# Half-unit products in the opening's pauses and a sixth projection unit among the row groups of a hybrid decoder block

## The chip, the cores and the metric

The kernel runs on one core of one Trainium2 chip. The metric is the device time of one execution in microseconds (us), smaller is better. Beside three timed executions there is one profiled execution, from which all durations of single instructions come. Engines are named as in the profile: PE (TensorE products), PEld (its weight loads), DVE (VectorE), ACT (ScalarE), POOL (GpSimd), SP (SyncE, whose queue issues nearly all loads).

## The reference

The block takes x (256 rows of 2048) and a condition vector c (2048), in float32. Cut to what matters here:

```
mod = silu(c) @ w_ada + b_ada                       # 6 vectors of 2048
sh1, sc1, g1, sh2, sc2, g2 = split(mod, 6)
h = rms_norm(x, norm_mix_g) * (1 + sc1) + sh1
u, q, k, v, ga, gb = split(h @ w_in, ...)           # 4 x 1024, then 2 x 2048
y_ssm = s5_branch(u, ...)                           # scan, gelu, sigmoid(y @ w_glu)
y_att = moba_attention(q, k, v, rel_bias)           # here plain causal, 8 heads of 128
merged = sigmoid(ga) * (y_ssm @ w_proj_ssm) + sigmoid(gb) * (y_att @ w_proj_attn)
x = x + g1 * (merged @ w_out)
h2 = rms_norm(x, norm_mlp_g) * (1 + sc2) + sh2
x = x + g2 * (square(relu(h2 @ w_ff1)) @ w_ff2)
out = rms_norm(x, norm_final_g)
```

## The kernel before, in words

**Products.** Every large product splits each operand into a rounded part (hi) and the rest (lo) and adds three products: hi·hi, hi·lo and lo·hi. A weight tile of 128 rows and 1024 columns (512 KB) is loaded into wraw (7 places), rounded by ACT into whi and subtracted by DVE into wlo (4 places each; `load`, `split` and `stream`, lines 148 to 182). `gemm_t` (L184) uses the weights as the stationary operand and makes transposed results, 24 products of 256 columns for each tile. `gemm_n` (L219) uses the activations as the stationary operand and makes 12 products of 512 columns. Each such unit of 1024 output columns takes four banks of PSUM; the main pool has five (tag mm), a second pool three (tag ax).

**The rows of h.** The 2048 rows of the transposed h come 128 at a time (kt 0 to 15). Each row tile needs its part of sh1 and sc1, that is 256 columns of w_ada. For kt 0 to 3 PE makes these sums from specially laid out tiles (`ada_first`, L247: adap, then adac). For kt 4 to 15 DVE multiplies rows of w_ada by the broadcast vector cb and sums them (`ada_wide`, L326, L342: 128x2048 each). The loads of those go into a ring of places, four at first, later two, because half of the ring's space is taken by the scan's tables. `scale1` and `make_h1` (L460 to L472) then make h, and split it into ah (hi and lo).

**Order.** The kernel writes its order by hand. A unit is one of u, q, k, v and the gate halves (ga, gb), over one or more row groups: GR = (4, 6, 6) row tiles. In the first group (4 tiles) the units q, k, v and u run; then the first half of ga over groups 0 and 1, then u, v, k over group 1, q over groups 1 and 2, ga's first half and u over group 2 (the loop over `qkvu`, L1118). After that come k and v over group 2, then the second half of ga and both halves of gb over all 16 tiles, in single units. Partial sums of a unit are copied out by ACT the first time and added by DVE later. In the opening, q's four tiles run one row at a time: between two of them the sums of the next row are made (`follow`, L989), and then `idle` (L124) issues 8 products of 256 columns into a tile called unread, while the next row of h is being made.

**Lanes.** After each weight tile `step` advances the lanes, lists of smaller jobs, each at a rate in jobs per tile: w_ada's remaining sums (lane ada; rates R1 to R4, RS0 to RS3, RPA, RWO, RM), the building of the scan's tables (lane ssm; it begins after SL steps, rates SR1 and SR2), attention and then the scan itself (lane m; RAT and RSS). `want` and `drain` pull jobs of the lane ada ahead where rows are needed. Within this order a planner puts instructions by their priority and its own estimate of when they are ready. Each engine then carries out its list in that order.

**Places.** The tile x holds the transposed input until all rows of h are made. Then its slot (X16) becomes ga, both halves. The attention scores (asc) use free columns of ga. The slot S3 holds uT, the u unit's result, which 32 small DMAs on POOL's queue re-lay into u (`hop_in`, L807); afterwards S3 holds the scan's states. The bias table tz of attention is loaded by 4 DMAs on the same queue (`bias_load`, L499). When the scan is done, 32 more DMAs (`hop_out`) bring its result into yT, which is split into yy (hi and lo) for the product with w_glu.

Of the kernel before, what the change touches and what calls it, by code (L numbers as in the profile page):

```python
# [12 lines left out]
F32 = mybir.dt.float32  # L13
F32R = mybir.dt.float32r
# [5 lines left out]
P = 128  # L20
# [22 lines left out]
SR1 = .27  # L43
# [3 lines left out]
SL = 18  # L47
R1 = .92
R2 = .56
R3 = .15  # L50
R4 = .5
RS0 = 1.0
RS1 = 1.0
RSM = .1
# [4 lines left out]
RSS = .37  # L59
RPA = .69  # L60
# [17 lines left out]
class Kern:  # L78
    def __init__(self, ctx, tc, a, out):
# [9 lines left out]
        self.last = self.gate = self.hgate = self.agate = None  # L89
        self.gates = []  # L90
# [33 lines left out]
    def idle(self, n):  # L124
        o = self.aux("unread")[:, 0:S]
        for _ in range(n):
            with self.after(self.adac):
                self.nc.tensor.matmul(o, self.whi[:, 0:P], self.whi[:, 0:S], start=True, stop=True)
# [35 lines left out]

    def stream(self, src, kts, c0, homes=()):
        homes = list(homes)
        for kt in kts:
            with self.tc.high_priority(offset=OFF):
                w = self.load(src, kt, c0)
                home = homes.pop(0) if homes else None  # L170
                if home:
                    hi, lo = home
                else:
                    hi = self.wp.tile([P, 1024], F32R, name="whi", tag="whi", bufs=4)
                    lo = self.wp.tile([P, 1024], F32R, name="wlo", tag="wlo", bufs=4)
                self.gate, self.hgate = self.gates.pop(0) if self.gates else (None, None)
                self.split(hi, lo, w)
                self.gate = self.hgate = None
            if not isinstance(kt, list):
                self.want(kt)  # L180
            yield kt, hi, lo
            self.step()
# [64 lines left out]
    def ada_first(self, j, kt, done, home=None, gate=None):  # L247
# [29 lines left out]
        def fold(gate=None):  # L277
# [3 lines left out]
            done(pc[:, 0:1])  # L281
# [622 lines left out]
    def body(self):  # L904
# [64 lines left out]
        with self.tc.high_priority(offset=OF1):  # L969
# [9 lines left out]
            self.make_h1(0, A1, B1, 1)  # L979
            self.gates = [(None, self.acopy)]  # L980
# [7 lines left out]

        def follow(kt):  # L989
            def f():  # L990
                with self.tc.high_priority(offset=OF1):
                    parts = modn(kt, homes[kt], (self.mid, self.mm))
# [3 lines left out]
                    self.scale1(kt, n=1)  # L996
                    totals(parts)
                    self.idle(8)
                    self.make_h1(kt, A1, B1, 1)
# [522 lines left out]
```

## Time and profile before

| | |
|---|---|
| timed executions | 1396.94, 1400.31, 1401.72 us; median 1400.31 |
| profiled execution | 1400.28 us; span 1398.5 us from first to last instruction |
| granted clock of TensorE, mean over the span | 0.997 |
| busy: PE, DVE, ACT | 98%, 76%, 50% of the span |
| idle before products for rows of h (ah), 22 to 300 us | 4.9 us in 4 waits |
| loaded from memory | 350.79 MB, 253 GB/s over the span |

A row of the timeline gives start, duration, engine, line, operation, out<-in and shape; in brackets stands how long the engine was idle before it and what ended that. Products overlap in PE's pipeline, so the time from one start to the next says more than the duration. A row of the waits gives who waited for whom, total us, times and the longest.

### The profile page before, as it was taken

Reading aid. Unit: us, or ns where it says so; the run is one execution under the profiler, and the core shown is the slowest. Engines: PE = TensorE matmul, PEld = TensorE weight load, DVE = VectorE, ACT = ScalarE, POOL = GpSimd, SP = SyncE. Lnnn points to the kernel's source line nnn. Section 1 sums busy time; section 2 is a strip of 40 time slices with the busy share of each in tenths; the row PEclk is TensorE's granted clock in tenths of the full one; section 3 lists DMA queues with packets and bytes.
Section 4 is the critical chain, followed back from the end, with each engine's and each line's share of the span. In section 5 each row is a group of like instructions: output and inputs, shape, how many; then the busy total and the mean of one; then the engine's idle time right before and its main releaser. Section 6 shows DMA issues by size and latency. Waiting matters only on the chain.

```text
span 1398.5 us, 22052 instructions
## 1 busy us (share of the span) xinstructions
PE 1365.9 (98%) x8584; PEld 1179.5 (84%) x8584; DVE 1062.1 (76%) x1485; ACT 701.7 (50%) x928; POOL 42.5 (3%) x95
## 2 busy tenths in 40 slices
PE   6999999999999999999999999999999999999997
PEld 5888988978788897888999888888888888888885
DVE  5799998888798888977886976767666454555677
ACT  4554444346646743445455664544453553635543
POOL 1000000400002200000000000000000000000000
PEclk9999999999999999999999999999999999999999
DMA  9999965889356889898597877798878666566552
GB/s 373 392 405 342 330 222 167 236 291 340 125 157 212 286 285 351 286 351 283 198 381 276 310 244 246 250 251 286 242 238 241 199 194 189 188 190 188 181 195 75
DMA packets 112425, 356.47 MB, mean 255 GB/s; under 512 B 12240, under 2 KB 12272, under 8 KB 111904
## 3 DMA queue, kind: packets, MB, share of 16 engines
q1 hardware_dynamic: 109280, 348.96, 73.6%
q0 software_dynamic: 2896, 5.83, 1.4%
q8 instruction: 67, 1.10, 0.3%
q14 instruction: 38, 0.31, 0.1%
q10 hardware_dynamic: 144, 0.26, 0.1%
HBM read 350.79 MB, written 2.51 MB: 253 GB/s over the span
## 4 chain that ended last, share of the span: by engine, by line
PE 88%; DVE 6%; DMA 3%; ACT 2%; issue 1%; SPq 0%; DVEq 0%; ACTq 0%
PE pn L239 16%; PE pn L240 15%; PE pn L241 15%; PE pd L213 13%; PE pd L215 7%; PE pt L196 5%; PE pt L197 5%; PE pt L198 5%; DVE wlo L161 2%; DMA wraw<-in_w_proj_ssm_dram 1%; DVE wraw L300 1%; ACT whi L159 1%; PE trv L668 1%; PE ys L886 1%; PE rk L702 1%
## 5 line engine op out<-in xcount | busy, mean ns | idle before, releaser
L159 ACT CAST whi<-wraw 128x1024 fp32r<-128x1024 f32 x448 | 467.6, 1051 | 564.8 <-PE pn L240 247.4
L161 DVE TENSOR_TENSOR wlo<-wraw,whi 128x1024 fp32r<-128x1024 f32 x448 | 544.7, 1221 | 250.9 <-ACT whi L159 243.2
L213 PE MATMUL pd<-h2h,whi 128*128 128x512 f32 x800 | 282.6, 398 | 0.0
L215 PE MATMUL pd<-h2h,wlo 128*128 128x256 f32 x800 | 224.2, 281 | 0.0
L239 PE MATMUL pn<-whi,ff 128*128 128x512 f32 x496 | 193.1, 389 | 0.0
L240 PE MATMUL pn<-whi,ff 128*128 128x512 f32 x496 | 193.0, 389 | 0.0
L241 PE MATMUL pn<-wlo,ff 128*128 128x512 f32 x496 | 191.7, 389 | 0.0
L213 PEld LDWEIGHTS pd<-h2h,whi 128*128 128x128 f32 x800 | 150.1, 188 | 37.1
L300 DVE SCALAR_TENSOR_TENSOR wraw<-wraw,cb 128x1024 f32<-128x1024 f32 x128 | 155.9, 1218 | 0.0
L215 PEld LDWEIGHTS pd<-h2h,wlo 128*128 128x128 f32 x800 | 151.1, 189 | 0.5
L239 PE MATMUL pn<-whi,ah 128*128 128x512 f32 x320 | 126.6, 398 | 2.5 <-ACT whi L159 1.6
L240 PE MATMUL pn<-whi,ah 128*128 128x512 f32 x320 | 125.4, 392 | 0.0
L241 PE MATMUL pn<-wlo,ah 128*128 128x512 f32 x320 | 114.6, 393 | 0.5 <-DVE wlo L161 0.5
L196 PE MATMUL pt<-ah,whi 128*128 128x256 f32 x384 | 106.0, 286 | 4.9 <-ACT ah L159 4.9
L241 PEld LDWEIGHTS pn<-wlo,ff 128*128 128x128 f32 x496 | 93.1, 188 | 19.5
L239 PEld LDWEIGHTS pn<-whi,ff 128*128 128x128 f32 x496 | 93.1, 188 | 19.4
L240 PEld LDWEIGHTS pn<-whi,ff 128*128 128x128 f32 x496 | 93.1, 188 | 19.2
L197 PE MATMUL pt<-ah,whi 128*128 128x256 f32 x384 | 107.9, 286 | 0.0
L198 PE MATMUL pt<-ah,wlo 128*128 128x256 f32 x384 | 103.4, 284 | 2.1 <-DVE wlo L161 2.1
L196 PEld LDWEIGHTS pt<-ah,whi 128*128 128x128 f32 x384 | 72.5, 192 | 6.5 <-ACT ah L159 5.8
L197 PEld LDWEIGHTS pt<-ah,whi 128*128 128x128 f32 x384 | 73.9, 192 | 1.6 <-issue 0.8
L198 PEld LDWEIGHTS pt<-ah,wlo 128*128 128x128 f32 x384 | 71.7, 193 | 2.7 <-DVE wlo L161 2.6
(376 smaller groups left out, 1981.3 us busy)
## 6 DMA issues: line engine op xcount, KB each, us to landing
wraw<-in_w_ff_dram SPq DMA_DIRECT2D x256, 512.0 KB, 4.7
wraw<-in_w_in_dram SPq DMA_DIRECT2D x128, 512.0 KB, 6.0
wraw<-in_wat_dram SPq DMA_DIRECT2D x128, 512.0 KB, 5.8
ahm<-in_wat_dram SPq DMA_DIRECT2D x48, 512.0 KB, 6.9
wraw<-in_w_out_dram SPq DMA_DIRECT2D x32, 512.0 KB, 6.5
wraw<-in_w_proj_attn_dram SPq DMA_DIRECT2D x16, 512.0 KB, 6.2
wraw<-in_w_proj_ssm_dram SPq DMA_DIRECT2D x16, 512.0 KB, 6.2
ahm<-in_wan_dram SPq DMA_DIRECT2D x8, 512.0 KB, 11.1
```

The costliest lines, as they stand in the source:

```text
L159: h = self.nc.scalar.copy(hi, src)
L161: s = self.nc.vector.tensor_sub(lo, src, hi.bitcast(F32))
L196: nc.tensor.matmul(o, hi[:, c], xh[:, kx, :], start=st, stop=False, skip_group_check=True)
L197: nc.tensor.matmul(o, hi[:, c], xl[:, kx, :], start=False, stop=False, skip_group_check=True)
L198: self.mm = nc.tensor.matmul(o, lo[:, c], xh[:, kx, :], start=False, stop=sp, skip_group_check=True)
L213: nc.tensor.matmul(banks[blk], hi[:, c], x2[:, :, kt, :], start=i + k == 0, stop=False, skip_group_check=True)
L215: self.mm = nc.tensor.matmul(banks[blk][:, S:2 * S], lo[:, c], x2[:, 0, kt, :], start=False, stop=i == n - 1 and k == 1, skip_group_check= ...
L239: nc.tensor.matmul(o, xh[:, kx, tk], hi[:, c], start=q == 0, stop=False)
L240: nc.tensor.matmul(o, xl[:, kx, tk], hi[:, c], start=False, stop=False)
L241: self.mm = last = nc.tensor.matmul(o, xh[:, kx, tk], lo[:, c], start=False, stop=q == n - 1)
L300: v.scalar_tensor_tensor(w, w, 1.0, self.cb[:, (i % 2) * 1024:(i % 2 + 1) * 1024], op0=OP.mult, op1=OP.mult, accum_out=pc[:, i:i + 1])
L668: nc.tensor.matmul(p[q, k * 64:(k + 1) * 64], self.VT[q, i, 8 * b + k, :], self.ident[q, q], start=True, stop=True)
```

## The change

- **Opening.** Each row's job first loads half a tile of w_in, columns 2048 to 2559 (the first half of k), for the row before. Its ACT rounding and DVE subtraction wait for the row before to be done; the step from the sums to A and B (`done`) waits for that subtraction. In place of the 8 unread products come the half tile's 12 products (`half_mul`), into two banks of their own, held over four rows. A fourth job, after the last row, does the half tile of row 3 and copies the result to qk. The unit k over group 0 is then a unit of half width (`gemm_h`, two banks, two tiles of w_in in one load), and the first two tiles of v are fetched before its results are copied out.
- **Sixth unit.** The second half of ga becomes a unit of the row groups: (5, 0, 0) before ga's first half, and (5, 1, 2) after v. Its partial sums lie in the first half of the tile x, once rows 0 to 7 of h are traced (`drain(4)`). ga is now a view of x, with the two halves apart.
- **Places.** The ring of w_ada's rows has four places for the first 16 of the 24 loads (12 before) and then two. The bp table waits for one more pair of rows (`drain(6)`).
- **Moved.** The scan's tables begin after 24 steps (18 before) and are flushed after k over group 2, not before it; the bias table is loaded after that. The scores move from ga to the slot S3, which uT had. `to_ssm` stays at the eighth tile of ga's second half, which now has 12 tiles. Rates of the lanes change.

```diff
-SR1 = .27
+SR1 = .35
-SL = 18
-R1 = .92
-R2 = .56
-R3 = .15
-R4 = .5
+SL = 24
+R1 = .8
+R2 = .62
+R3 = .0
+R4 = .65
-RS1 = 1.0
-RSM = .1
+RS1 = .9
+RSM = .2
-RSS = .37
-RPA = .69
+RSS = .4
+RPA = .74
...
-    def idle(self, n):
-        o = self.aux("unread")[:, 0:S]
-        for _ in range(n):
-            with self.after(self.adac):
-                self.nc.tensor.matmul(o, self.whi[:, 0:P], self.whi[:, 0:S], start=True, stop=True)
+    def half_load(self, src, kt, c0):
+        w = self.wp.tile([P, 1024], F32, name="wraw", tag="wraw", bufs=7)[:, 0:512]
+        with self.after(self.last):
+            self.last = self.nc.sync.dma_start(w, src[kt * P:(kt + 1) * P, c0:c0 + 512])
+        hi = self.wp.tile([P, 1024], F32R, name="whi", tag="whi", bufs=4)[:, 0:512]
+        lo = self.wp.tile([P, 1024], F32R, name="wlo", tag="wlo", bufs=4)[:, 0:512]
+        return kt, w, hi, lo
+
+    def half_mul(self, banks, half, st, sp):
+        nc = self.nc
+        kt, w, hi, lo = half
+        with self.after(self.adac):
+            for blk in range(4):
+                o = banks[blk // 2][:, (blk % 2) * S:(blk % 2 + 1) * S]
+                c = slice(blk * P, (blk + 1) * P)
+                nc.tensor.matmul(o, hi[:, c], self.ah[:, kt, :], start=st and blk % 2 == 0, stop=False,
+                                 skip_group_check=True)
+                nc.tensor.matmul(o, hi[:, c], self.al[:, kt, :], start=False, stop=False, skip_group_check=True)
+                nc.tensor.matmul(o, lo[:, c], self.ah[:, kt, :], start=False, stop=sp, skip_group_check=True)
...
-            done(pc[:, 0:1])
+            with self.after(self.half_lo):
+                done(pc[:, 0:1])
...
-            self.drain(5)
+            self.drain(6)
...
         def follow(kt):
             def f():
                 with self.tc.high_priority(offset=OF1):
+                    half = self.half_load(win, kt - 1, 2048)
+                    if kt == 1:
+                        hb.extend([self.bank("ph0"), self.aux("ph1")])
+                    if kt == 4:
+                        self.gate, self.hgate = self.row_done
+                        self.split(half[2], half[3], half[1])
+                        self.gate = self.hgate = None
+                        self.half_mul(hb, half, False, True)
+                        for b in range(2):
+                            nc.scalar.copy(self.qk[:, 1, 2 * b:2 * b + 2, :], hb[b].rearrange("p (k s) -> p k s", s=S))
+                        return
...
                     self.scale1(kt, n=1)
+                    self.gate, self.hgate = self.row_done
+                    self.half_lo = self.split(half[2], half[3], half[1])
+                    self.gate = self.hgate = None
                     totals(parts)
-                    self.idle(8)
+                    self.half_mul(hb, half, kt == 1, False)
                     self.make_h1(kt, A1, B1, 1)
+                    self.row_done = self.done[-1]
...
+        def g2_evac(banks, add):
+            self.drain(4)
+            for b in range(4):
+                d = self.ga[:, 0, b // 2, (b % 2) * 512:(b % 2) * 512 + 512]
+                if add:
+                    v.tensor_add(d, d, banks[b])
+                else:
+                    nc.scalar.copy(d, banks[b])
...
-        ring = wide * 3 + wide[2:4] * 6
+        ring = wide * 4 + wide[2:4] * 4
...
-        for u in ((0, 0, 0), (1, 0, 0), (2, 0, 0), (3, 0, 0), (4, 0, 1), (3, 1, 1), (2, 1, 1), (1, 1, 1), (0, 1, 2),
+        for u in ((0, 0, 0), (1, 0, 0), (2, 0, 0), (3, 0, 0), (5, 0, 0), (4, 0, 1), (3, 1, 1), (2, 1, 1), (1, 1, 1), (0, 1, 2),
                   (4, 2, 2), (3, 2, 2)):
...
         self.hop_in()
+        self.lanes["ada"][1] = R4
+        qkvu(1, 2, 2)
         self.flush("ssm")
-        self.lanes["ada"][1] = R4
         self.bias_load()
-        qkvu(1, 2, 2)
         qkvu(2, 2, 2)
         ga = self.ga
-        self.asc = ga[:, :, 1024:1792]
+        self.asc = self.slot("S3", [P, 2, 768], name="asc")
...
+        qkvu(5, 1, 2, {8: to_ssm})
+        for i in range(2):
+            self.lanes["ada"][1] = (RSM, RS2)[i]
+            banks = self.gemm_n(win, range(KT), 6144 + 1024 * i, self.ah, self.al)
```

More of the change, by code (lines that the diff above doesn't have):

```diff
@@ new lines, in gemm_h @@
+    def gemm_h(self, src, kts, c0, xh, xl):
+        nc = self.nc
+        banks = [self.bank(f"pt{b}") for b in range(2)]
+        pairs = self.pairs(list(kts))
+        n = len(pairs)
+        for i, (ks, hi, lo) in enumerate(self.stream(src, pairs, c0)):
+            for k, kt in enumerate(ks):
+                for blk in range(4):
+                    o = banks[blk // 2][:, (blk % 2) * S:(blk % 2 + 1) * S]
+                    c = slice(512 * k + blk * P, 512 * k + (blk + 1) * P)
+                    nc.tensor.matmul(o, hi[:, c], xh[:, kt, :], start=i + k == 0 and blk % 2 == 0, stop=False,
+                                     skip_group_check=True)
+                    nc.tensor.matmul(o, hi[:, c], xl[:, kt, :], start=False, stop=False, skip_group_check=True)
+                    self.mm = nc.tensor.matmul(o, lo[:, c], xh[:, kt, :], start=False, stop=i == n - 1 and k == 1,
+                                               skip_group_check=True)
+        return banks
@@ L163, in split, with fetch @@
         return s
+    def fetch(self, src, kt, c0, home=None):
+        with self.tc.high_priority(offset=OFF):
+            w = self.load(src, kt, c0)
+            if home:
+                hi, lo = home
+            else:
+                hi = self.wp.tile([P, 1024], F32R, name="whi", tag="whi", bufs=4)
+                lo = self.wp.tile([P, 1024], F32R, name="wlo", tag="wlo", bufs=4)
+            self.gate, self.hgate = self.gates.pop(0) if self.gates else (None, None)
+            self.split(hi, lo, w)
+            self.gate = self.hgate = None
+        return hi, lo
     def stream(self, src, kts, c0, homes=()):
@@ L167, in stream @@
         for kt in kts:
[L168 to L180, printed above, removed]
+            if self.pre and self.pre[0][0:2] == (kt, c0):
+                hi, lo = self.pre.pop(0)[2:]
+            else:
+                hi, lo = self.fetch(src, kt, c0, homes.pop(0) if homes else None)
+            self.want(kt[1] if isinstance(kt, list) else kt)
             yield kt, hi, lo
@@ L1035, in g_evac @@
         def g_evac(banks, add):
-            if add:
-                self.ga = self.slot("X16", [P, 2, D], name="ga")
-            else:
+            if not add:
                 gpart["p"] = self.slot("S4", [P, 2, 1024], name="gp")
@@ L1067, in body, with qkvu @@
                           + mod2(1) + mod2(2) + mod2(3))
-        def qkvu(which, g0, g1):
+        def qkvu(which, g0, g1, mid={}):
             kts = range(groups[g0][0], sum(groups[g1]))
-            if which < 2:
+            if which == 1 and g0 == 0:
+                banks = self.gemm_h(win, kts, 2560, self.ah, self.al)
+                for kt in kts[0:2]:
+                    self.pre.append((kt, 3072) + self.fetch(win, kt, 3072))
+                for b in range(2):
+                    with self.after(self.done[-1][1]):
+                        nc.scalar.copy(self.qk[:, 1, 4 + 2 * b:6 + 2 * b, :],
+                                       banks[b].rearrange("p (k s) -> p k s", s=S))
+            elif which < 2:
                 qk_evac(which, self.gemm_t(win, kts, 1024 + 1024 * which, self.ah, self.al), g0)
```

34 lines of the change are left out of this document (19 added, 15 removed).

## The prediction

> **What bounds the kernel now.** I read the page first, then the waits of PE, the windows by stage, and the timelines of the opening.
>
> ```profile
> span 1398.5 us, 22052 instructions
> PE 1365.9 (98%) x8584; PEld 1179.5 (84%) x8584; DVE 1062.1 (76%) x1485; ACT 701.7 (50%) x928; POOL 42.5 (3%) x95
> ```
> ```profile
> 22.00:50.00 28.00, 25.53 (x318) 21.92 (x319) 12.11 (x50) 10.38 (x20) 0.51 (x1) 0.94 1.03 408
> 50.00:110.00 60.00, 57.91 (x352) 51.70 (x351) 59.17 (x68) 34.26 (x47) 1.31 (x2) 1.00 1.02 393
> 110.00:200.00 90.00, 89.11 (x643) 83.73 (x643) 81.74 (x96) 39.53 (x46) 0.00 (x0) 1.00 0.89 317
> ```
> ```profile
> PE pt L196 <- ACT ah L159: 4.9, 4, 3.5
> PE pt L198 <- DVE wlo L161: 2.1, 1, 2.1
> PE pn L239 <- ACT whi L159: 1.6, 2, 1.2
> PE pn L241 <- DVE wlo L161: 0.5, 1, 0.5
> ```
> The columns of the windows are length, then busy time of PE, PEld, DVE, ACT and POOL, granted clock, DMA share and GB/s. PE is busy in 1365.9 of 1398.5 us, so a change that leaves the products as they are can win only what PE waits, what it spends on products that nobody reads, and what it then doesn't lose elsewhere. The waits shown are those from 22 to 300 us, the stage that the change rebuilds: 4.9 us for the rows of h in the opening (3.5 of them once, ahead of the first row), and 2.1 + 1.6 + 0.5 us later. From 50 to 110 us VectorE is busy in 59.17 of 60 us and the DMA engines are full (1.02, 393 GB/s): there VectorE and DMA stand nearly as close to the end as PE does.
>
> **The pauses of the opening.** One row in the timelines of PE and ACT:
>
> ```profile
> 32.05 0.74 PE L196 MATMUL pt<-ah,whi 128*128 128x256 f32 x4 [0.45 <-ACT ah L159]
> ...
> 37.51 0.84 PE L280 MATMUL adac<-s 128*128 128x1 f32 x4
> 38.21 1.19 PE L128 MATMUL unread<-whi 128*128 128x256 f32 x8
> 39.85 0.75 PE L196 MATMUL pt<-ah,whi 128*128 128x256 f32 x4 [0.45 <-ACT ah L159]
> 50.69 0.28 PE L198 MATMUL pt<-ah,wlo 128*128 128x256 f32 x1
> 50.81 0.28 PE L196 MATMUL pt<-ah,whi 128*128 128x256 f32 x1
> ```
> ```profile
> 37.81 1.05 ACT L159 CAST whi<-wraw 128x1024 fp32r<-128x1024 f32 x1
> 38.76 0.60 ACT L470 ACTIVATE htmp<-xt,B,A 128x256 f32<-128x256 f32 x1
> 39.39 0.40 ACT L159 CAST ah<-htmp 128x256 fp32r<-128x256 f32 x1
> ```
> After a row's sums (adac) PE runs 8 products into a tile called unread, then waits 0.45 us for the next row of h, which comes over ACT (scale at 38.76, rounding at 39.39). From the first unread product at 38.21 to the next useful one at 39.85 are 1.64 us, and the next row's pause looks the same. Products of 256 columns start 0.12 us apart (50.69, 50.81). The change takes the 8 out and puts 12 useful ones there (four blocks, three products each): 12 x 0.12 = 1.44 us, which fits into 1.64. There are three such pauses; the fourth half tile comes after the last row and is only moved. So 3 x 12 x 0.12 = **4.3 us** of the k unit's products leave the path. The bound below is 0, if the pause grows by what is put into it; the bound above is 3 x 1.64 = 4.9 us, if it closed wholly.
>
> What the filling adds: per row one ACT rounding and one VectorE subtraction of 512 columns, half of a 1.05 us cast and of a 1.22 us one (rows at 37.81 above and 108.51 below), an estimate of 0.5 and 0.6 us. The scale step must now wait for that subtraction. It may start once the row before is done (ACT at 39.79), some 6 us ahead of the sums, while ACT and VectorE are busy in 10.38 and 12.11 of 28 us. I take 0; if the half tile were late, 1.1 us for each row would stand on the chain. The four half tiles are SP loads of 256 KB ahead of the next row's w_ada tiles; at 408 GB/s one takes 0.64 us, 2.6 us in all by the last. The waits show no DMA that PE waited for up to 300 us, so this is covered; without the cover it costs up to 2.6 us, and the k unit then has 1 MB less to load.
> The Trainium skill ("DMA: Bandwidth & Descriptors", Anatomy of one DMA) speaks against halves: a transfer costs about 2 us and its bytes over 436 GB/s. Paid one by one, an estimate from that page is 2.6 us for 256 KB against 1.6 for half of 512 KB, 4 x 1.0 = 4 us more, which would eat the gain. The 408 GB/s of the first window, one 512 KB tile every 1.3 us, says that the fixed part overlaps here, and I go by the row.
>
> **The sixth unit among the row groups.** Four tiles of the second gate half (ga) are pulled ahead of the unit that first needs rows 4 to 9, and the other 12 come after the row groups.
>
> ```profile
> 86.35 0.62 ACT L1031 COPY uT<-pt 128x512 f32<-128x512 f32 x1
> ...
> 95.71 1.06 ACT L159 CAST whi<-wraw 128x1024 fp32r<-128x1024 f32 x1 [1.96 <-PE pn L240]
> 98.43 1.06 ACT L159 CAST whi<-wraw 128x1024 fp32r<-128x1024 f32 x1 [1.66 <-PE pn L240]
> ```
> ```profile
> 79.60 0.68 DVE L161 TENSOR_TENSOR ah<-htmp,ah 128x512 fp32r<-128x512 f32 x1
> ...
> 103.29 0.68 DVE L631 TENSOR_TENSOR tt<-cmp,fr 128x512 f32<-128x512 f32 x1
> ...
> 108.51 1.22 DVE L161 TENSOR_TENSOR wlo<-wraw,whi 128x1024 fp32r<-128x1024 f32 x1
> 109.65 0.68 DVE L632 TENSOR_TENSOR tt<-cmp,fr 128x512 f32<-128x512 f32 x1
> ```
> ```profile
> 109.78 0.38 PE L198 MATMUL pt<-ah,wlo 128*128 128x256 f32 x1 [2.09 <-DVE wlo L161]
> 196.28 0.50 PE L239 MATMUL pn<-whi,ah 128*128 128x512 f32 x1 [0.37 <-ACT whi L159]
> 197.54 0.50 PE L241 MATMUL pn<-wlo,ah 128*128 128x512 f32 x1 [0.53 <-DVE wlo L161]
> ```
> A tile of 512-wide products takes PE 2.72 us (95.71 to 98.43), so four give 10.9 us; PE comes 4.3 us sooner from the pauses, so rows 4 to 9 are due 6.6 us later than now. VectorE has four more tiles to split by then, 4 x 1.22 = 4.9 us, which leaves it 1.7 us better. The scan's build steps that lie in front of the late tile (four of them, the first at 103.29 and the last at 109.65, 4 x 0.68 = 2.7 us) go back too: their lane starts 24 steps in and not 18. Together 4.4 us against the 2.1 us that PE waited at 109.78, so this wait should go. Of the two short ones near 197 (0.37 and 0.53 us) the same slack, and four places in place of two for four more of w_ada's row loads, should take most. I book **-2.5** of the 3.0 us. Bounds: -3.0, and +4.3 if VectorE, which had 0.83 us to spare in 60, meets the earlier PE with no slack at all. The 1.2 us near 295 stays booked as it is, since w_ada's rate there rises (.5 to .65).
>
> The old x tile now takes the sixth unit's partial sums, so their third bank may only be copied out once rows 4 and 5 of x are read. Five banks serve two units of four, so the next unit would wait for that copy. Those rows were finished at 79.60, and the bank is due when the unit ends: u, the unit ahead of it, has its last bank copied at 86.35 now, so 86 + 10.9 - 4.3 = 92.6 us. That is 13 us of cover, cost 0; with w_ada's rate cut from .92 to .8 the cover may shrink, hardly below 0.
>
> **Attention and scan.** What is moved here is the danger.
>
> ```profile
> 300.00:360.00 60.00, 57.33 (x277) 47.33 (x277) 44.35 (x77) 39.28 (x79) 0.00 (x0) 1.00 0.73 266
> ```
> ```profile
> PE pav L782 <- ACT ga L775: 1.7, 1, 1.7
> PE pn L239 <- ACT ga L1166: 1.0, 1, 1.0
> ```
> ```profile
> 277.95 0.38 DVE L758 SCALAR_TENSOR_TENSOR ga<-sco,tz 128x128 f32<-128x128 f32 x1
> ```
> ```profile
> 259.16 4.77 POOL L807 DMA_DIRECT2D u<-uT  x10 [6.38 <-DVE uT L1029]
> 281.36 1.07 POOL L807 DMA_DIRECT2D u<-uT  x2 [1.69 <-DMA u<-uT]
> ```
> ```profile
> tz<-scr POOLq DMA_DIRECT2D x4, 256.0 KB, 5.2
> u<-uT POOLq DMA_DIRECT2D x32, 32.0 KB, 5.5
> ```
> ```profile
> L807 POOL DMA_DIRECT2D yT<-u x32: 484/484/487, 443.6 to 465.7; - x32
> L159 ACT CAST yy<-yT x4: 1130/1150/1157, 478.5 to 481.3; 128x512 fp32r<-128x512 f32 x4
> L196 PEld LDWEIGHTS pt<-yy,whi x64: 188/192/192, 482.4 to 505.1; 128*128 128x128 f32 x64
> ```
> The scores (asc) move from ga into the slot of uT. So attention's first write must now wait for the last of the 32 copies out of uT: they are issued from 259.2 to 282.4 (281.36 + 1.07) and the last lands 5.5 us later, at 287.9, while attention now begins at 277.95. In the changed kernel uT is ready 10.9 - 4.3 - 2.5 = 4.1 us later, so attention starts no sooner than 292, 14 us later than now. The four loads of the bias table (tz) are also issued after the next unit, on POOL's queue, perhaps behind the 32 copies: about as much as four of the copies, 2 us of issue, and 5.2 us to land. Behind the waiting instruction on VectorE stand the splits of w_in's tiles, for which PE waits. On the other end, the scan's result lands at 465.7 + 0.5 + 5.1 = 471.3 us and is first read at 478.5: 7.2 us of slack, and the four fewer tiles after attention take no work from the chain. Its lanes are paced by tiles: from the eighth tile of the gate unit the scan's 14 jobs take 14/.37 = 37.8 tiles now and 14/.4 = 35 then, 7.6 us less. Start 4 us later by the tiles, some 3 to 9 us lost with attention, up to 7.6 us won back by the pace: 0 to 6 us late against 7.2 us of slack, less the 6 us by which PE comes sooner. I book **+1.0**; the ends are 0 and +13 (14 + 6 - 7.2).
>
> The sixth unit's sums are added by VectorE at its end, four adds in place of four copies on ACT; VectorE is busy in 44 of the 60 us there, so 0. The other rates only spread w_ada's remaining sums over stages with room on VectorE: 0, with 1 us to either side.
>
> **Sum.** The profiled execution took 1400.28 us, 1.8 more than its span, and stands on the median of 1400.31. -4.3 - 2.5 + 1.0 = -5.8: **1394.5 us**. About 0.3%, 4.2 us, is what a measurement can tell here, so the forecast lies just beyond it.
>
> **Rivals.**
> 1. *VectorE keeps the gain.* The pauses fill, but PE meets VectorE's backlog sooner and gives most of the 4.3 us back before 112 us; nothing or 1 us is won of the later waits, new ones of 1 us come. For it: 59.17 of 60 us busy. Against: 10.9 us of new cover against 4.9 us of work. 1400.3 - 4.3 + 2.3 = 1398, between 1396 and 1401. Chance 0.20.
> 2. *Attention and scan come late* (the other side). If the 14 us pass down the chain to yy, the scan's gate product (pt<-yy) starts 14 + 6 - 7.2 = 13 us after PE could: 1394.5 - 1.0 + 13 = 1406; with half of the delay passed, 7 + 6 - 7.2 = 5.8 us, 1399. It decides from a delay of 8 us passed on, where the loss of 8 + 6 - 7.2 = 6.8 us eats the whole gain. For it: the landing of the copies and the 7.2 us. Against: attention's later heads ran at VectorE's pace, and the lanes are paced by tiles. The Trainium skill ("TensorE: Matmul & The Clock Gate", Architectural detail) has ACT and VectorE work strictly in order, so that a score that waits for tz or uT also holds the splits behind it. By that rule this costs PE directly at 290 us; no row so far shows VectorE pass a waiting instruction. Chance 0.14, 1401 to 1408.
> 3. *The change doesn't fill the pause.* The half tile's split comes late on ACT and VectorE, each pause grows by 1.1 us, and 3.3 of the 4.3 us go: 1397.8. Chance 0.05; nothing in the 28 us window speaks for it.
> 4. *More than forecast:* also the 1.2 us near 295 and the 1.7 + 1.0 us of attention's waits between 300 and 360 go: 1394.5 - 1.0 - 3.9 = 1389.6. Chance 0.05.
>
> **Numbers.** The forecast itself, 1391 to 1397, has 0.56. Faster by over 4.2 us: 0.52 of it, all of the fourth, 0.04 of the first: 0.61. Within: 0.04 + 0.15 + 0.04 = 0.23. Slower: 0.14 + 0.02 of the others = 0.16. The range goes from 1389.5 to 1403: it leaves out a half of the second rival and little else.
>
> **What would show it.** Right: no unread products; 12 products between adac and the next row's first, with the rows still 7.8 us apart (32.05 to 39.85 now); k's end some 4.3 us sooner; no wait of 2 us for wlo near 114 us. Wrong: rows over 8.5 us apart; VectorE idle before the first score near 290 with PE waiting for whi or wlo; a wait before the first pt<-yy near 475 us; a wait of the unit after the new one for a bank.

## The result, and the profile after

The changed kernel is **slower**: 1413.3 us median of 4 runs (1411.4 to 1415.7) against 1399.7 of the kernel before, ratio 1.010 with a 95% interval of 1.0073 to 1.0126. Its profiled execution took 1411.77 us. The forecast of 1394.5 and its range to 1403 are missed, on the side of the second rival and beyond its 1408.

From the page of the changed kernel:

```profile
span 1410.0 us, 22009 instructions
PE 1367.3 (97%) x8560; PEld 1182.7 (84%) x8560; DVE 1067.3 (76%) x1491; ACT 702.4 (50%) x930; POOL 42.7 (3%) x95
```

PE has 24 products fewer and is busy 1.4 us longer, in a span that is 11.5 us longer. The opening did what was forecast. PE's timeline there:

```profile
32.57 0.74 PE L234 MATMUL pt<-ah,whi 128*128 128x256 f32 x4
...
38.01 0.84 PE L318 MATMUL adac<-s 128*128 128x1 f32 x4
38.71 0.36 PE L141 MATMUL ph<-ah,whi 128*128 128x256 f32 x1
...
40.11 0.28 PE L144 MATMUL ph<-ah,wlo 128*128 128x256 f32 x1
...
40.35 0.74 PE L234 MATMUL pt<-ah,whi 128*128 128x256 f32 x4
```

The half tile's products (ph) run from 38.71 to 40.11 where the unread ones ran, and the rows still follow each other by 7.8 us (32.57 to 40.35). From the first product with h to the first product of v, the unit behind k, PE took 39.4 us before (22.9 to 62.3) and takes 34.9 us now (23.5 to 58.4; the rows that show these starts stand further down): by then 4.5 us are won. The loss is later. PE's waits in the changed kernel, the six longest in sum:

```profile
PE ys L925 <- DVE gc L1115: 5.1, 1, 5.1
PE pt L234 <- ACT ah L192: 4.5, 2, 3.2
PE rk L741 <- ACT tt L731: 4.4, 1, 4.4
PE pt L235 <- DVE yy L194: 2.9, 1, 2.9
PE ys L925 <- DVE sri L910: 2.7, 2, 2.0
PE pt L234 <- ACT yy L192: 1.9, 1, 1.9
```

The 2.1 us for wlo near 110 us are gone. New are a wait for the scan's tables (rk), waits for the scan's states (ys) and waits for its split result (yy). (The first row names gc, a short VectorE step. The products that waited read sri, which VectorE had written just before gc.) The 4.5 us for ah are 3.2 ahead of the first row and 1.4 near 206 us. Three windows of the changed kernel, then of the kernel before (columns as in the prediction: length, busy PE, PEld, DVE, ACT, POOL, granted clock, DMA share, GB/s):

```profile
200.00:260.00 60.00, 52.23 (x720) 46.44 (x719) 54.90 (x67) 24.20 (x33) 0.09 (x1) 0.97 0.37 112
420.00:460.00 40.00, 32.11 (x451) 26.29 (x447) 38.44 (x58) 16.59 (x24) 4.19 (x9) 0.87 0.23 71
460.00:520.00 60.00, 55.19 (x318) 48.95 (x317) 47.19 (x60) 38.55 (x45) 11.17 (x24) 0.94 0.84 284
```
```profile
200.00:260.00 60.00, 60.00 (x790) 53.63 (x790) 55.06 (x67) 23.22 (x30) 2.80 (x6) 1.00 0.53 160
420.00:460.00 40.00, 40.00 (x342) 33.45 (x341) 31.79 (x40) 26.67 (x35) 11.46 (x24) 1.00 0.68 211
460.00:520.00 60.00, 60.00 (x357) 53.62 (x356) 52.51 (x68) 38.30 (x48) 3.82 (x8) 1.00 0.85 291
```

Before, PE was never idle in these windows; now it lacks 7.8, 7.9 and 4.8 us. And the clock falls: 0.87 over 40 us is the same as 10 us at half rate, 0.94 over 60 us as 7 us.

**A table by stage.** Four marks cut each profile: the first product with h, the last pt<-ah (the end of k over the last row group: "rows"), the last pn<-whi,ah (the end of gb: "scan", in which attention and scan run beside the products) and the first pn<-whi,gg ("yy", with the split of the scan's result). They are read from the views of the tiles ah and gg, whose rows give first and last start. Before, then after:

```profile
L196 PE MATMUL pt<-ah,whi x384: 274/283/415, 22.9 to 273.0; 128*128 128x256 f32 x192
L239 PE MATMUL pn<-whi,ah x320: 387/389/580, 62.3 to 460.1; 128*128 128x512 f32 x160
```
```profile
L239 PE MATMUL pn<-whi,gg x64: 389/389/504, 527.4 to 574.4; 128*128 128x512 f32 x64
```
```profile
L234 PE MATMUL pt<-ah,whi x352: 274/283/582, 23.5 to 285.0; 128*128 128x256 f32 x176
L277 PE MATMUL pn<-whi,ah x320: 387/389/794, 58.4 to 468.6; 128*128 128x512 f32 x160
```
```profile
L277 PE MATMUL pn<-whi,gg x64: 387/389/499, 543.2 to 588.6; 128*128 128x512 f32 x64
```

The change moves four tiles, 10.9 us, from "scan" to "rows". Booked so, the kernel before has 261.0 us of rows and 176.2 us of scan:

| us | start | rows | scan | yy | rest | span |
|---|---|---|---|---|---|---|
| before, four tiles moved | 22.9 | 261.0 | 176.2 | 67.3 | 871.1 | 1398.5 |
| forecast | 22.9 | 254.2 | 177.2 | 67.3 | 871.1 | 1392.7 |
| after | 23.5 | 261.5 | 183.6 | 74.6 | 866.8 | 1410.0 |

So 6 to 7 us are missing in each of the three stages, and 4.3 come back after them. Part of these 4.3 is the spread of single profiles: four kernels of the next section whose products behind these marks are those of the kernel before show 868.2 to 869.0 us of rest, not 871.1. What wins the other 2 is open.

### The profile page after: what moved, and what is told of

It reads as the page before. It is cut to its first block, busy times and chain, and to the rows that moved or that the text cites. A ratio compares the mean times of both kernels' runs of the same rounds, so it can differ in the third digit from the quotient of the medians.

```text
span 1410.0 us, 22009 instructions
## 1 busy us (share of the span) xinstructions
PE 1367.3 (97%) x8560; PEld 1182.7 (84%) x8560; DVE 1067.3 (76%) x1491; ACT 702.4 (50%) x930; POOL 42.7 (3%) x95
## 4 chain that ended last, share of the span: by engine, by line
PE 86%; DVE 8%; ACT 3%; DMA 1%; issue 1%; SPq 0%; ACTq 0%; DVEq 0%
PE pn L277 15%; PE pn L278 15%; PE pn L279 15%; PE pd L251 13%; PE pd L253 7%; PE pt L235 5%; PE pt L234 5%; PE pt L236 5%; DVE wlo L194 2%; ACT whi L192 1%; PE rk L741 1%; DVE rw L904 1%; DMA wraw<-in_w_proj_ssm_dram 1%; PE trv L707 1%; DMA wraw<-in_w_proj_attn_dram 1%
## 5 line engine op out<-in xcount | busy, mean ns | idle before, releaser
L251 PEld LDWEIGHTS pd<-h2h,whi 128*128 128x128 f32 x800 | 149.9, 188 | 35.9
L234 PE MATMUL pt<-ah,whi 128*128 128x256 f32 x352 | 98.1, 288 | 5.0 <-ACT ah L192 4.5
L235 PE MATMUL pt<-ah,whi 128*128 128x256 f32 x352 | 99.7, 286 | 0.0
L236 PE MATMUL pt<-ah,wlo 128*128 128x256 f32 x352 | 96.7, 285 | 0.0
L277 PEld LDWEIGHTS pn<-whi,ah 128*128 128x128 f32 x320 | 60.8, 190 | 15.3 <-DVE qk L1069 1.1
L234 PEld LDWEIGHTS pt<-ah,whi 128*128 128x128 f32 x352 | 66.9, 194 | 7.4 <-ACT ah L192 5.5
L279 PEld LDWEIGHTS pn<-wlo,ah 128*128 128x128 f32 x320 | 60.4, 190 | 13.9 <-DVE wlo L194 1.4
```

The source lines that it names most:

```text
L234: nc.tensor.matmul(o, hi[:, c], xh[:, kx, :], start=st, stop=False, skip_group_check=True)
L235: nc.tensor.matmul(o, hi[:, c], xl[:, kx, :], start=False, stop=False, skip_group_check=True)
L236: self.mm = nc.tensor.matmul(o, lo[:, c], xh[:, kx, :], start=False, stop=sp, skip_group_check=True)
L251: nc.tensor.matmul(banks[blk], hi[:, c], x2[:, :, kt, :], start=i + k == 0, stop=False, skip_group_check=True)
L277: nc.tensor.matmul(o, xh[:, kx, tk], hi[:, c], start=q == 0, stop=False)
L279: self.mm = last = nc.tensor.matmul(o, xh[:, kx, tk], lo[:, c], start=False, stop=q == n - 1)
```

## The experiments

Three theories stood at first: (1) the places of w_ada's rows; (2) the scores in uT's slot, which hold attention and scan back; (3) four tiles fewer after attention, so less cover for the scan. The second round added (4): the scan's tables, begun later, crowd with the last rows. The later runs added yy's place in the lists of ACT and VectorE, the half clock, and the worth of the filled pauses. All ratios are to the kernel before, run beside it on the same chip (its medians were 1398.4 to 1400.0 us). Scores "over q and k" means that each head's scores are written over its own q and k, which nothing reads after them.

| kernel | us | ratio, 95% interval | rows | scan | yy | rest |
|---|---|---|---|---|---|---|
| b_halves | 1402.0 | 1.0008 (0.9996 to 1.0019) | 249.6 | 192.5 | 67.3 | 869.0 |
| b_places | 1399.3 | 0.9994 (0.9981 to 1.0007) | 248.6 | 187.4 | 67.4 | 868.7 |
| b_asc_s3 | 1408.2 | 1.0049 (1.0031 to 1.0067) | 251.0 | 194.1 | 67.4 | 868.3 |
| b_qk | 1399.3 | 0.9994 (0.9982 to 1.0006) | 250.0 | 185.7 | 67.4 | 868.2 |
| a_places_back | 1414.1 | 1.0094 (1.0075 to 1.0113) | 264.7 | 184.0 | 73.2 | 867.2 |
| a_qk | 1401.9 | 1.0012 (1.0000 to 1.0024) | 262.2 | 175.1 | 72.1 | 867.6 |
| a_sl18 | 1413.2 | 1.0095 (1.0072 to 1.0118) | 259.7 | 178.5 | 77.7 | 872.4 |
| a_qk_sl18 | 1403.1 | 1.0021 (1.0008 to 1.0034) | 259.7 | 175.2 | 71.2 | 871.1 |
| a_qk_rates | 1410.7 | 1.0071 (1.0045 to 1.0098) | 257.9 | 181.8 | 78.6 | 868.5 |
| a_qk_rss5 | 1412.2 | 1.0090 (1.0072 to 1.0108) | 263.4 | 184.3 | 70.4 | 868.8 |
| a_qk_nohalf | 1412.3 | 1.0093 (1.0075 to 1.0111) | 262.5 | 174.4 | 77.9 | 872.6 |
| a_warm | 1418.0 | 1.0127 (1.0111 to 1.0142) | 266.5 | 185.2 | 74.0 | 866.5 |
| a_yy | 1410.5 | 1.0078 (1.0061 to 1.0094) | 263.7 | 183.6 | 68.2 | 869.7 |
| a_qk_yy | 1401.8 | 1.0016 (1.0003 to 1.0029) | 263.6 | 175.6 | 67.8 | 870.5 |
| a_qk_yy_nohalf | 1409.1 | 1.0069 (1.0054 to 1.0084) | 262.6 | 176.6 | 67.2 | 877.2 |
| a_sl21 | 1401.1 | 1.0018 (1.0006 to 1.0030) | 253.1 | 180.2 | 70.0 | 871.5 |
| a_qk_sl21 | 1396.6 | 0.9984 (0.9974 to 0.9994) | 253.6 | 175.1 | 71.8 | 871.0 |
| a_qk_yy_sl21 | 1394.7 | 0.9964 (0.9951 to 0.9977) | 254.9 | 175.1 | 70.3 | 870.3 |

Those with b_ are built from the kernel before and have its stages (250.1 and 187.1 without the moved tiles), those with a_ from the changed one. A stage's time is of one profile; three kernels that should have the rows of the changed kernel (a_qk, a_yy, a_qk_yy) show 262.2, 263.7 and 263.6 against its 261.5, so about 2 us mean nothing. All the intervals in the table lie within 2% of the kernel before.

**The parts alone, in the kernel before.**

b_halves takes the opening's part of the change alone (half_load, half_mul, gemm_h, the order in follow):

```diff
-                    self.idle(8)
+                    self.half_mul(hb, half, kt == 1, False)
```

> The kernel before with the half-tile products of the opening alone (half tile loads, 12 products in each pause, k over group 0 in half width); units, places, slots and rates as before. Theory 1 (places): w_ada's row loads keep the slot of the bp table longer, so the scan's tables are built late. Theory 2 (scores): attention waits for the copies out of uT. Theory 3 (cover): four tiles fewer after the row groups leave attention and scan without products to hide behind. All three leave this part alone: 4 us faster, 1395.4. If the pause's gain is lost again downstream whatever the rest, the time stays at 1399.7.

b_places takes the four places for 16 loads and the later bp:

```diff
-        ring = wide * 3 + wide[2:4] * 6
+        ring = wide * 4 + wide[2:4] * 4
-            self.drain(5)
+            self.drain(6)
```

> The kernel before with four places for the first 16 of w_ada's row loads and the bp table waiting for one more pair of rows; all else as before. Theory 1 (places): bp is first written near 200 us and not at 144, the build steps are crowded, PE waits 4 us or more for rk near 240, and the time rises by 6 to 12 us, to 1406 to 1412. Theories 2 (scores) and 3 (cover): within 2 us of 1399.7.

b_asc_s3 moves the scores alone:

```diff
-        self.asc = ga[:, :, 1024:1792]
+        self.asc = self.slot("S3", [P, 2, 768], name="asc")
```

> The kernel before with the scores in the slot of uT; all else as before. Theory 2 (scores): the first score moves from 278 us to 290 or later, the scan's result comes 10 us or more later, and the time rises by 5 to 12 us, to 1405 to 1412. Theories 1 (places) and 3 (cover): within 2 us of 1399.7, since four tiles more lie behind than in the changed kernel.

b_qk is the control for the kernels with the scores over q and k:

```diff
-        s = self.asc[:, h % 2, 0:384]
+        s0, s1 = qT[:, 0:P], kT
```

> Control: the kernel before, with the scores written over each head's own q and k and the transposed weights copied out in two pieces (as in the changed kernel with that place), nothing else. If that place is free of cost, it runs within 0.3% of the kernel before (1396 to 1404 us, likeliest 1400), and the 1402 us of the changed kernel with the same place hold the rest of the change alone. If the two pieces and the added ACT copies cost something themselves, 3 to 6 us more, and the rest of the change is worth that much more than it seemed.

The places cost and win nothing; nor does the other place of the scores. The scores in uT's slot cost 0.49% by themselves, 7.0 us of it in the stage "scan" (194.1 against 187.1). The filled pauses alone win nothing that can be measured in the whole. Their products are in place, and v's first product comes 34.8 us after the first with h, 4.6 us sooner than before. But the rows' stage is only 0.5 us shorter: PE waits further down. In the transposed units (pt) it waits 4.7 us for wlo from 22 to 300 us, where before it waited 2.1. The longest of these waits, 3.6 us, lies at 108 us with 3.4 us at half clock behind it, and 1.1 us for rk are new. The stage "scan" is 5.4 us longer, with 6.8 us at half clock at 296 us; what makes it longer stays open. Those waits for wlo in b_halves:

```profile
PE pt L236 <- DVE wlo L194: 4.7, 3, 3.6
```

**The parts taken out of the changed kernel.**

a_places_back has the places as before (the diff of b_places, reversed).

> The changed kernel with the places as before (four for the first 12 loads, bp one pair of rows earlier); halves, sixth unit, slots and rates as changed. Theory 1 (places): bp is written some 50 us earlier, the 4.4 us wait for rk and the late uT go, and 6 to 9 us come back: 1404 to 1407. Theories 2 (scores) and 3 (cover): at most 2 us come back, 1411 to 1413.

a_qk has the scores over q and k (the edit of b_qk, and no slot S3).

> The changed kernel, but each head's scores and transposed weights are written over that head's own q and k, so no score waits for uT's copies (the transposed weights are copied in two pieces instead of one). Theory 2 (scores in uT's slot): the first score comes before 292 us instead of 310, the waits for the scan's steps (423 to 452) and for yy (491) shrink to under 3 us together, 6 to 9 us come back, 1404 to 1407. Theory 3 (four tiles fewer behind the row groups): the scan stays short of cover, at most 3 us come back, over 1410.

a_sl18 has the tables' start as before, a_qk_sl18 both, a_qk_rates the whole block of rates as before beside the scores over q and k:

```diff
-SL = 24
+SL = 18
-SR1 = .35
+SR1 = .27
```

> The changed kernel with the build lane's start and first rate as before (18 steps, .27). Theory 4 (late builds): the build steps begin before 120 us and not at 142, the 4.4 us wait for rk goes with the half-clock stretch behind it, uT is ready some 5 us sooner, and 5 to 8 us come back: 1405 to 1408. Theory 2 alone: at most 2 us, 1411 to 1413.

> Both edits of the two kernels before this one: scores over q and k, and the build lane's start and first rate as before. If theories 2 and 4 hold and their waits are separate, the gains add up: 12 to 16 us back, 1397 to 1401. If theory 3 holds, it stays above 1404.

> The changed kernel with scores over q and k and with the whole block of rates as before. It asks whether the new rates carry part of the loss. Theories 2 and 4: as the kernel with both edits, 1397 to 1401, since the other rates count for little. If the other new rates are what the new order needs (w_ada's sums then come in the wrong stages), it is over 3 us slower than that one.

Theory 1 fell. Theory 2 held on this side too: with another place for the scores "scan" goes from 183.6 to 175.1, and 12 of the 13.6 us are back. Theory 4 seemed to fall: with 18 steps the tables' first step runs at 105.9 us in place of 142.1, but the waits for rk only go from 4.4 to 3.6 us in sum, a wait of 2.4 us near 116 us comes back (the tables now crowd with rows 4 to 9) with half clock behind it, and "rows" wins only 2 us. The rates of the changed kernel are no ornament. The kernel that differs from a_qk_rates in the other rates alone is a_qk_sl18, and against it "scan" is 6.6 us and yy 7.4 us longer. Which of these rates does it was not shown. Theory 3 would put it on the pace of the scan's lane (.37 before, .4 now). A pace faster still loses, as the next kernel shows.

a_qk_rss5 sets the lane to .5.

```diff
-RSS = .4
+RSS = .5
```

> The changed kernel with the scores over q and k and the scan's lane at .5 jobs for a tile in place of .4: its 14 jobs take 28 tiles in place of 35. If the lane's pace sets when the scan's result comes (yT's last copies at 469 us, yy at 484), yT comes some 15 us sooner, the 2.1 us wait at yy and its 3.4 us at half clock go, 3 to 4 us sooner in all: 1398 us. If VectorE and ACT set the scan's pace, yT comes no more than 5 us sooner and the time stays at 1402; PE's waits for the scan's tables (2.5 us now) then grow to 5 us or more.

yT's last copy came 10 us sooner (458.7 against 468.9 us), as the first case has it, and PE's waits for ys grew from 1.4 to 7.2 us, as the second has it: "scan" is 9 us longer. So .5 is too fast; between .4 and .5 nothing was run.

**Half clock.** In the changed kernel 20 us between 240 and 510 us run at half clock, each stretch behind or around a wait of 1.9 to 5.1 us: 3.4 us at 248, 3.4 at 426, 6.8 at 436, 6.8 at 494. PE's timeline there shows it in the starts, 0.21 us apart and not 0.12:

```profile
496.93 0.58 PE L235 MATMUL pt<-yy,whi 128*128 128x256 f32 x1 [2.89 <-DVE yy L194]
497.31 0.41 PE L236 MATMUL pt<-yy,wlo 128*128 128x256 f32 x1
497.53 0.41 PE L234 MATMUL pt<-yy,whi 128*128 128x256 f32 x1
497.74 0.41 PE L235 MATMUL pt<-yy,whi 128*128 128x256 f32 x1
```

a_warm puts products that nobody reads ahead of three of the waits:

```diff
+    def warm(self, p, n):
+        with self.after(self.mm):
+            for _ in range(n):
+                self.nc.tensor.matmul(p[:, 0:S], self.ah[:, 0, 0:P], self.ah[:, 0, :], start=True, stop=True)
```

> The changed kernel with products that nobody reads put ahead of three long waits of PE: 32 ahead of the first rk (4.4 us of waiting), 36 ahead of the third group of ys (5.1 us), 14 and 22 around the first product of yy (1.9 and 2.9 us). They fit into the waits, so the waits' ends stay. If the stretches at half clock behind these waits (3.4 us at 248, 6.8 at 436, 6.8 at 494) come from PE having stood idle, they go, and the 1.7 us behind rk and the 2 us behind yy are won, those behind ys in part: 1408 to 1410 against 1413. If the clock falls for another reason, the stretches stay, and the time too.

It was 5 us slower. Its timeline of PE:

```profile
238.21 4.00 PE L130 MATMUL rk<-ah 128*128 128x256 f32 x32
...
247.00 0.48 PE L754 MATMUL rk<-cc,tt 64*64 64x64 f32 x4 [4.43 <-ACT tt L742]
...
498.72 1.83 PE L130 MATMUL pt<-ah 128*128 128x256 f32 x14
500.85 2.80 PE L130 MATMUL pt<-ah 128*128 128x256 f32 x22
```

Ahead of rk they did not land in the wait. Between the tables' last transposes (trv) and rk the changed kernel runs 56 products with h, this one 24 and the 32 that nobody reads: 32 useful products were pushed behind rk. The end of the wait is set by VectorE's table steps and stays (rk comes 224.5 us after the first product with h, 224.4 in the changed kernel), so the wait did not shrink (4.43), its half clock stayed, and "rows" is 5 us longer. Ahead of the third ys the 36 do lie in the wait, which is gone, but the next group then waits 2.6 us, with 3.4 us at half clock where 6.8 were. At yy they lie in the wait, and the stretch at half clock behind it is gone. So the stretch follows PE's idleness. The stage yy is only 0.6 us shorter for it.

What half clock costs can be read in the opening, where the kernels have either 3.4 us of it (granted clock 0.94 from 22 to 50 us) or 6.8 us (0.88) over the same products. From the first product with h to the first of v, the kernels with filled pauses take 34.7 to 34.9 us with 3.4 us of it and 35.9 to 36.2 with 6.8; with unread products they take 39.2 to 39.4 and 40.4 to 40.5. So 3.4 us at half clock cost about 1.2 us there. The filled pauses win about 4.5 us by that point with either.

**yy's place.** The expectation that the scan's landing holds yy was still the prediction's. The views of yT and yy in the changed kernel speak against it:

```profile
L846 POOL DMA_DIRECT2D yT<-u x32: 487/487/489, 455.8 to 474.7; - x32
L192 ACT CAST yy<-yT x4: 1105/1140/1143, 492.1 to 494.9; 128x512 fp32r<-128x512 f32 x4
...
DMA to landing us min/median/max: 1.8/4.1/6.5
```

The last copy is issued by 475.2 and lands by 481.7, and ACT takes the first split 10 us later, behind three tiles of w_glu. a_yy and a_qk_yy put yy ahead of the second tile on ACT and ahead of the products gb on VectorE:

```diff
+        self.gates = [(None, None)] * 1 + [(None, hold[1])]
         banks = self.gemm_t(a["w_glu"][0], range(8), 0, yy[:, 0], yy[:, 1])
...
-                v.tensor_mul(d, d, banks[b])
+                with self.after(None if cg else hold[2]):
+                    v.tensor_mul(d, d, banks[b])
```

> The changed kernel with yy's splits put ahead on ACT (behind the first tile of w_glu, the second waits for them) and on VectorE (the products gb of the unit before wait for them). The scan's result has landed near 480 us there, yy's first split starts at 492. If the place of yy in ACT's and VectorE's lists makes PE wait, both waits at yy go (1.9 and 2.9 us) and the 6.8 us at half clock behind them, which cost some 2 to 3 us: 1405 to 1408 against 1413. If the landing of the scan's result sets it, the waits stay and so does the time.

> The same put ahead in the changed kernel with the scores over q and k. By the order of the lists the wait at yy (2.1 us) and its 3.4 us at half clock go: 1398 to 1399 against 1402. By the landing (474.7 us there) nothing: 1402.

The waits at yy went in both (4.8 us but for 0.4 in the first, and 1.4 us in three pieces in the second, where 2.1 were expected), and so did the half clock behind them; the stage yy goes from 74.6 to 68.2 and from 72.1 to 67.8. So the place in the lists made these waits, not the landing. The end won less, 2.4 us in the first, within its interval, and nothing in the second: about 3 us more stand in the rest.

**The pauses in the changed kernel.** a_qk_nohalf and a_qk_yy_nohalf take the filled pauses out (the diff of b_halves, reversed).

> The changed kernel with the scores over q and k, and with the opening of the kernel before: 8 unread products in the pauses, k's first unit in full width. If the pauses' 4.3 us stay won in the changed kernel, this is 4 us slower than with them: 1406. If they are given back to VectorE's and ACT's backlog further down (the waits at 203 to 206 and at 246 us, and half clock behind them), it is the same within 0.2% of 1402, with those waits shorter by 3 to 4 us in sum.

> That kernel with the opening of before (unread products, k in full width). If the 10 us by which the kernel without filled pauses was slower were mostly its waits at yy (6.2 us and 10.2 us at half clock), and not the pauses, this is only the pauses' 4.3 us slower than the one above: 1402 to 1404. If they come from the pauses, 1408 to 1410.

Both are slower, by 10 and by 7 us, and neither theory has it right: the rows' stage is the same with and without filled pauses (262.5 and 262.6 against 262.2 and 263.6), so the 4.5 us that the pauses win by v are given back within it. The difference stands in yy (for the first: 5.8 us of waiting there and 10.2 us at half clock) and in the rest (4.4 and 5.6 us of waits after 528 us against 2.2 in a_qk_yy). Taking them out also changes how many steps the lanes get; whether that is the cause of the loss in yy and in the rest stays open.

**The tables' start again.** 18 and 24 steps each crowd one end. a_qk_yy_sl21, a_sl21 and a_qk_sl21 take 21:

```diff
-SL = 24
+SL = 21
-SR1 = .35
+SR1 = .31
```

> That kernel with the scan's tables begun after 21 steps at .31 (18 at .27 before, 24 at .35 changed). If the tables' start can be put so that neither the wait near 116 us (2.6 us with 18) nor those at 203 to 206 and for rk (3.3 and 4.4 us with 24) come at full size, 2 to 4 us are won: 1395 to 1397. If the waits only change places, 1398 to 1400 as the one with 24.

> The changed kernel with the scan's tables begun after 21 steps at .31, all else as it is (scores in uT's slot, yy in its place). If the tables' start is a cause of its own, the waits at 203 to 206 and for rk go here too and 5 to 7 us are won: 1406 to 1408 against 1413; the waits for ys and at yy stay. If it pays only where attention isn't late, as with 18 steps, 1412 to 1414.

> The changed kernel with the scores over q and k and the tables begun after 21 steps at .31, yy in its place. If yy's place costs nothing by itself (0.1 us between the two kernels that differ in it alone), 1394 to 1396, as with yy put ahead. If the earlier PE meets yy's place in the lists, 2 to 4 us of the 7 go there again: 1397 to 1399.

With this alone 11 of the 13.6 us are back (a_sl21): the tables' first step runs at 116.0 us, there is no wait for rk, and the rows' stage is 253.1 us. With the scores over q and k beside it the kernel is faster than before, by 0.16% (0.06 to 0.26), and with yy put ahead by 0.36% (0.23 to 0.49), 1394.7 us: it **beats both**, the kernel before and the changed one. That yy's place bears on it isn't settled, since the two intervals overlap. The windows of a_qk_yy_sl21, and its rows of the tile ah:

```profile
200.00:260.00 60.00, 58.54 (x792) 53.53 (x791) 56.12 (x68) 26.88 (x36) 1.97 (x4) 1.00 0.47 141
420.00:460.00 40.00, 37.05 (x323) 29.61 (x322) 32.42 (x42) 26.87 (x36) 13.88 (x29) 1.00 0.64 191
460.00:520.00 60.00, 59.73 (x355) 53.23 (x354) 55.02 (x70) 35.76 (x44) 1.44 (x3) 1.00 0.87 302
```
```profile
L234 PE MATMUL pt<-ah,whi x352: 274/283/580, 22.8 to 277.7; 128*128 128x256 f32 x176
L277 PE MATMUL pn<-whi,ah x320: 387/389/586, 58.8 to 452.8; 128*128 128x512 f32 x160
```

All three windows have the full clock again and most of their PE time: 1.5, 3.0 and 0.3 us are lacking where 7.8, 7.9 and 4.8 were.

## Why the prediction was wrong

**The pauses, -4.3, and the late waits, -2.5.** The pauses did what was forecast: rows 7.8 us apart, and 4.5 us won when v begins. The wait of 2 us near 110 is gone too. But the sum of the two needs "rows" to fall from 261.0 to 254.2 us, and it was 261.5. The step that failed is the one that put the tables' later start on the credit side: "The scan's build steps that lie in front of the late tile [...] go back too: their lane starts 24 steps in and not 18." It asked what leaves the stretch before 110 us and not where it goes. The first of these steps ran at 103.29 us before and runs 39 us later now:

```profile
142.06 0.68 DVE L670 TENSOR_TENSOR tt<-cmp,fr 128x512 f32<-128x512 f32 x1
```

So the work goes behind 200 us, where VectorE must make the last rows of h and the tables at once. The short waits near 197, which the -2.5 counts as mostly gone (0.9 us), are there 2.7 us in three pieces, and 4.4 us for rk come behind them. PE's timeline of the changed kernel, at the last rows and at the first rk:

```profile
203.97 0.49 PE L279 MATMUL pn<-wlo,ah 128*128 128x512 f32 x1 [0.99 <-DVE wlo L194]
205.82 0.74 PE L234 MATMUL pt<-ah,whi 128*128 128x256 f32 x4 [1.35 <-ACT ah L192]
```
```profile
247.93 0.33 PE L741 MATMUL rk<-cc,tt 64*64 64x64 f32 x4 [4.44 <-ACT tt L731]
```

With 21 steps in place of 24 (and the rate that goes with them) the same opening gives 253.1 to 254.9 us, the forecast's 254.2. So the sum of the first two terms was right in size for a start at 21, and at 24 the whole 6.8 us are taken back. The first rival, VectorE's backlog, names the mechanism, but it books 2.3 us for it in all and places most of it before 112 us. In the kernel before it has the place right too: b_halves waits 3.6 us for wlo at 108 us where 2.1 were.

**Attention and scan, +1.0.** The mechanism was named and its size was wrong: "I book +1.0; the ends are 0 and +13." The slot alone costs 7.0 us in the kernel before, 8.5 in the changed one (183.6 to 175.1), 5.1 with the tables at 21 (180.2 to 175.1). Three parts of the working failed.
- uT was to be ready 10.9 - 4.3 - 2.5 = 4.1 us later. The first copy out of it is issued 12 us later, at 271.14 in place of 259.16, since the two gains are not there by then. The bias table (tz), which the prediction saw perhaps behind the copies, comes ahead of them and holds nothing up. POOL's timeline in the changed kernel:

```profile
259.91 1.97 POOL L545 DMA_DIRECT2D tz<-scr  x4 [123.32 <-PE rk L741]
271.14 4.79 POOL L846 DMA_DIRECT2D u<-uT  x10 [9.26 <-DVE uT L1086]
...
291.01 1.56 POOL L846 DMA_DIRECT2D u<-uT  x3 [0.92 <-DMA u<-uT]
```

- The prediction counted the first score from the landing of the last copy, 292 us, and looked for VectorE idle before it with PE waiting. The last copies are issued by 292.6 and land by 300 (at most 7.4 us later in this profile), and the score comes at 310. VectorE did not stand idle for it. Its timeline in the changed kernel:

```profile
292.75 1.23 DVE L194 TENSOR_TENSOR wlo<-wraw,whi 128x1024 fp32r<-128x1024 f32 x1 [3.32 <-ACT whi L192]
...
308.31 1.22 DVE L339 SCALAR_TENSOR_TENSOR wraw<-wraw,cb 128x1024 f32<-128x1024 f32 x1
...
310.02 0.39 DVE L797 SCALAR_TENSOR_TENSOR asc<-sco,tz 128x128 f32<-128x128 f32 x1 [0.21 <-issue]
```

Its idle times there (3.3 us ahead of 292.75) end with a rounding on ACT, not with a copy. The planner had put the score behind other work, at 310 in place of 278; in a_qk, whose score needn't wait, it comes at 291.8. So the strict order of an engine's list, which the prediction weighed from the Trainium skill, had nothing to bite on: no row shows splits held behind a waiting score, and PE is busy in all of the 60 us from 300 to 360. The delay went into the jobs behind it instead. In b_asc_s3, where nothing else differs, the first pav is at 322.2 and not at 296.8.
- The slack of 7.2 us was measured from the landing of yT to yy's first split, as if the landing released yy. Its place in ACT's and VectorE's lists does (a_yy). The other loss came before it, in "scan", where PE waited for the states that its products ys read (5.1 and 2.7 us) and then ran at half clock. The prediction had booked no price for a late scan on PE itself. The second rival, this danger's other side, has the cause right and the path wrong: it lets the delay reach PE at yy or near 290 us, not in the scan's own products.

**Half clock** stands nowhere in the sum, and a wait can cost more than its length by it: by the 1.2 us for 3.4 us that the opening shows, the 20 us after 240 us would be 7 us, an estimate and rather too high, since parts of these stretches lie within the waits. The Trainium skill ("TensorE: Matmul & The Clock Gate", Part 1) has the clock at half rate after an idle window of some 3.4 us, and at full rate again after a busy one. The traces agree as to the lengths, 3.4 and 6.8 us, and as to the cause (a_warm at yy). They differ as to when: three waits of 1.4 us in sum at yy in a_qk had 3.4 us behind them too.

**The two causes overlap.** Alone, the other place of the scores brings 12 us and the earlier tables 11, both together 15 (from 13.6 us slower than before to 1.8 faster). By the stages, the tables alone win the rows (8.4 us; the scores 0), and the scores win most of "scan" (8.5 us; the tables 3.4, both 8.5). The two meet at the scan and at yy, where each takes away waits that the other would: at yy 4.8 us fall to 1.4 with the scores moved and to none with the tables at 21, at ys 7.8 us fall to 1.4 and to 5.8.

**Costed right:** the places (0), the 256 KB loads (0: the opening's rows kept their pace, and the 4 us that were weighed against halves did not come), the fifth bank (no wait of the sixth unit's next unit for a bank). Neither the third rival (pauses not filled) nor the fourth (more than forecast) came. The other rates were booked at 0 with 1 us to either side. They matter: with those of before a_qk_sl18 is 7.6 us slower.

## What to carry to other kernels

When a change moves background work later, find what is made in the stretch where it now lands, and book that stretch too; a credit at one end with no debit at the other is half a sum. When a buffer's old user must drain first, look for the cost in everything that is scheduled after the new first write, since a planner hides the wait as a later place in a list; and read a slack from what releases the reader, its list included, and not from when the data land. A table by stage, with the same marks in every run, shows which of three losses an edit has removed, where the total alone (a_sl18, a_qk_nohalf) misleads. And an early gain has to be followed to the end: here 4.5 us stood won at 58 us and were gone at 285.

## What the runs showed of the hardware

- Half clock came in stretches of 3.4 or 6.8 us (10.2 twice, in a_qk_rates and a_qk_nohalf), and not only behind long waits: 1.4 us of waiting in three pieces at yy in a_qk, and 1.8 and 1.5 us at ys in a_sl21, had 3.4 us of it behind them, while three waits of 2.7 us in sum at 202 to 206 us had none in the changed kernel and 6.8 us in a_qk.
- 3.4 us at half clock cost about 1.2 us in the opening (34.8 against 36.0 us for the same products).
- Four loads of 256 KB in the opening did not slow the rows, which stayed 7.8 us apart, at 405 GB/s from 22 to 50 us.
